# Down and w_out with tokens on the partitions: Strassen over 16 of 22 row blocks, norms along rows

## The chip, the cores and the metric

The kernel runs on one core of one Trainium2 chip. TensorE (PE) multiplies, VectorE (DVE) and ScalarE (ACT) work on tiles in SBUF and PSUM, GpSimd (POOL) helps, and SyncE (SP) and other engines' queues issue transfers (DMA). The metric is the device time of one execution in microseconds (us). The kernel before takes 2519.57 us, the median of 3 runs (2518.89 to 2524.14).

## The reference

Two layers of an encoder on 512 tokens with 1024 channels. Each layer has three sub-layers, and each of these has a norm ahead of it and one behind it:

```python
    for l in range(L):
        y = swiglu(rmsnorm(h, ffn1_pre_g[l]), ffn1_w_gu[l], ffn1_w_down[l])
        h = h + 0.5 * rmsnorm(y, ffn1_post_g[l])
        u = rmsnorm(h, mix_pre_g[l])
        proj = u @ w_in[l]
        ...
        merged = jnp.sum(gates * yb, axis=2)
        h = h + rmsnorm(merged @ w_out[l], mix_post_g[l])
        y = swiglu(rmsnorm(h, ffn2_pre_g[l]), ffn2_w_gu[l], ffn2_w_down[l])
        h = h + 0.5 * rmsnorm(y, ffn2_post_g[l])
```

`swiglu(x)` is `(silu(gate) * up) @ w_down`, where gate and up are the halves of `x @ w_gu`, 2816 columns each. The mixer between the FFNs projects to three kinds of attention with a sigmoid gate per branch and channel, and ends with `w_out`, 1024 by 1024. All is float32.

## The kernel before

Everything is kept transposed: features on the partitions, 512 tokens along the free axis. So h is 8 tiles of 128x512 and an FFN's activations are 22 such row blocks. A product with weights has the weight block (128x128) as the stationary operand and the activation (512 tokens) as the moving one. To keep float32 accuracy, each operand is split into a high part that TensorE takes exactly and a low rest, and each product is three matmuls (hi x hi, hi x lo, lo x hi; lines L246 to L248, `mm3`, and L650 in `product`).

Weights come from DRAM in the order of use as tiles of 512 KB (8 blocks of 128x128, tag `wr`, 3 buffers). `ensure` splits them, high by ScalarE (L201), low by VectorE (L202), 512 columns an instruction.

An FFN begins with 6 plain columns of gate and up (`PLAIN`), whose first 3 accumulators run in two token halves (`begin`), so that they can start when half of the tokens are ready. The other 16 of the 22 columns are Strassen products: the 8 input blocks and 512 tokens are cut in two each way, and seven products of 12 matmuls of 128x256 (L650) take the place of eight. Their weight sums are VectorE's (L543, L562, L572 and others). Down follows: 8 columns of 22 row blocks, seven whole (512 tokens) and the last in two token halves (`end`).

The norm behind it goes over features, and so over partitions: squares are summed on POOL and VectorE (L311), a matmul with ones sums the partitions (L291), the root and reciprocal make one number per token, and `spread` (L282) repeats it on all partitions by a matmul with the identity. `refresh` multiplies y by it (L413), adds y to h (L416, POOL and VectorE) and makes the next operand X (L316, L317) without the next norm, whose factor `rB` is multiplied in later (for instance L1051 at the gates). The first half of the tokens does this under the second half's products. w_out does the same, with 2 columns in halves. During the mixer h lies in DRAM (`kept`).

The order on each engine is that of a list scheduler of the framework, which takes the program's order and the buffers that are free. Tags name the buffers: `wr` raw weights, `x` split weights, `mm`, `at`, `o` PSUM banks.

Of the kernel before, what the change touches and what calls it, by code (L numbers as in the profile page):

```python
# [16 lines left out]
P = 128  # L17
# [12 lines left out]
TAIL_MIX = 2  # L30
AHEAD = 2
WARM = 9
PLAIN = 6
PAD = {"f": 184, "m": 184}
SECOND = 1
MIX_HOLD = ("g", "g", "g", "g", "g", "tx")[-TAIL_MIX * KD // 4 :]
KEEP_FF = 16
TAIL_FF = KF - KEEP_FF
PAD_FF = -TAIL_FF % 4
NBLOCKS = L * (  # L40
    2 * (2 * KF * KD + KF * KD + TAIL_FF + PAD_FF) + 54 * KD + 3 * 4 * KD + KD * KD
)
# [20 lines left out]
ROWN = ("diff_lambda_q1", "diff_lambda_k1", "diff_lambda_q2", "diff_lambda_k2", "sw_sink")  # L63
ROWW = 4 * 64 + 8
# [47 lines left out]
def encoder_kernel(ctx: ExitStack, tc: tile.TileContext, order, xT, wts, cols, rows, rpb, consts, tables, out):  # L112
# [9 lines left out]
    BUFS = {"h": 8, "x": 12, "t": 6, "wr": 3, "wp": 4}  # L122
    ABUFS = {"f": {}, "m": {"rr": 4, "tx": 5, "st": 16, "g": 10, "s": 2, "pt": 4}}
# [35 lines left out]
    nhalf = cp.tile([P, NCOLS], F32, tag="nhalf", name="nhalf")  # L159
# [46 lines left out]
    def wblk(name, l, r, c):  # L206
        n = len(order)
        if n % HB == 0:
            upto = n // HB + 1 + AHEAD
            if n // HB < stream["limit"]:  # L210
                upto = min(upto, stream["limit"])
            ensure(upto)
            for _ in range(min(stream["pace"], len(stream["later"]))):
                stream["later"].pop(0)()
            stream["tile"] = stream["ready"].pop(0)
        order.append((name, l, r, c))
        hi, lo = stream["tile"]
# [3 lines left out]
    h = [big("h", name="h") for _ in range(KD)]  # L221

    def load(hs, *bs):
        for b in bs:
            nc.sync.dma_start(h[b][:, hs], xT[b * P : (b + 1) * P, hs])

    G.memset(ones, 1.0)
    nc.scalar.dma_start(colt, cols)
    A.activation(dummy, ones[:, 0:1], AF.Copy)
    load(HALVES[0], 0)  # L230
    fetch(2, nc.sync)
    load(HALVES[0], 1, 2)
    fetch(1, nc.sync)
    load(HALVES[0], 3, 4, 5)
    fetch(1, nc.sync)
    load(HALVES[0], 6, 7)
    load(HALVES[1], *range(KD))
    nc.sync.dma_start(cons, consts)
    warm = bank("o")
    for _ in range(WARM):  # L240
        PE.matmul(warm[:, :P], ones, ones, start=True, stop=True)
    V.tensor_scalar(out=half, in0=colt, scalar1=0.5, scalar2=None, op0=ALU.mult)
    V.tensor_scalar(out=nhalf, in0=colt, scalar1=-0.5, scalar2=None, op0=ALU.mult)

    def mm3(acc, w, x, start, stop):
        PE.matmul(acc, w[0], x[0], start=start, stop=False)  # L246
        PE.matmul(acc, w[0], x[1], start=False, stop=False)  # L247
        PE.matmul(acc, w[1], x[0], start=False, stop=stop)  # L248

    def dense(blocks, X, tags=("mm",), cs=WHOLE, accs=None, ws=None, midway=None):  # L250
        accs = accs or [bank(tags[i % len(tags)]) for i in range(len(blocks))]
        n = len(X)
        kept = []
        for k in range(n):
            if midway and k == n // 2:
                midway()
            x = X[k][0][:, cs], X[k][1][:, cs]
            for i, (acc, (name, l, r0, c)) in enumerate(zip(accs, blocks)):
                w = ws[k * len(blocks) + i] if ws else wblk(name, l, r0 + k, c)
                kept.append(w)  # L260
                mm3(acc[:, cs], w, x, k == 0, k == n - 1)
        return (accs, kept) if cs == HALVES[0] else accs
# [49 lines left out]

    def operand(X, i, b, gcol):
        hs = HALVES[i]
        hi, lo = X[b]
        A.activation(hi[:, hs], h[b][:, hs], AF.Copy, scale=gcol(b))  # L316
        V.scalar_tensor_tensor(  # L317
            out=lo[:, hs], in0=h[b][:, hs], scalar=gcol(b), in1=f(hi)[:, hs], op0=ALU.mult, op1=ALU.subtract
        )

    def begin(refresh, X, first, spare):

        s = Squares()
# [869 lines left out]
```

## Time and profile before

| | |
|---|---|
| runs (median, range) | 2519.57 us, 2518.89 to 2524.14 |
| profiled execution | 2517.49 us, its span 2515.7 us |
| mean granted TensorE clock | 0.994 |
| busy: TensorE, VectorE, ScalarE, POOL | 98%, 68%, 50%, 8% of the span |
| layer 0, FFN1: gate and up by Strassen | about 75 to 240 us |
| its down product, its handover | about 240 to 360, 360 to 375 us |
| mixer | about 375 to 910 us |
| weight tiles | 415 of 512 KB, 3.5 us from issue to landing |

Row forms of the profile: a group's row gives line, engine, operation, output<-inputs, shape, count, then busy us and mean ns, then the idle time of the engine ahead of it and what ended it. A timeline row gives start and duration in us. A row of windows gives the stretch, its width, then busy us of each engine, the granted clock (PEclk, 1.00 is full), the share of the DMA engines and GB/s.

### The profile page before, as it was taken

Reading aid. Unit: us, or ns where it says so; the run is one execution under the profiler, and the core shown is the slowest. Engines: PE = TensorE matmul, PEld = TensorE weight load, DVE = VectorE, ACT = ScalarE, POOL = GpSimd, SP = SyncE. Lnnn points to the kernel's source line nnn. Section 1 sums busy time; section 2 is a strip of 40 time slices with the busy share of each in tenths; the row PEclk is TensorE's granted clock in tenths of the full one; section 3 lists DMA queues with packets and bytes.
Section 4 is the critical chain, followed back from the end, with each engine's and each line's share of the span. In section 5 each row is a group of like instructions: output and inputs, shape, how many; then the busy total and the mean of one; then the engine's idle time right before and its main releaser. Section 6 shows DMA issues by size and latency. Waiting matters only on the chain.

```text
span 2515.7 us, 38188 instructions
## 1 busy us (share of the span) xinstructions
PE 2471.4 (98%) x14586; PEld 2181.1 (87%) x14586; DVE 1702.3 (68%) x3062; ACT 1260.5 (50%) x2447; POOL 197.6 (8%) x177
## 2 busy tenths in 40 slices
PE   9999999999999999999999999999999999999998
PEld 8999888888778889998889998888787788899987
DVE  8877248857767478773388772588676764887723
ACT  6555245645555455553355553546455554555532
POOL 0000020000111120000100000200011112100002
PEclk9999999999999999999999999999999999999999
DMA  4333337434443323333233333374344423233232
GB/s 153 109 106 97 100 101 208 115 109 127 117 126 98 108 65 116 101 101 93 92 93 109 110 93 93 125 197 116 107 126 133 119 90 110 65 116 103 91 103 84
DMA packets 97398, 278.21 MB, mean 111 GB/s; under 512 B 13504, under 2 KB 17984, under 8 KB 97216
## 3 DMA queue, kind: packets, MB, share of 16 engines
q10 hardware_dynamic: 41184, 149.52, 19.5%
q1 hardware_dynamic: 56032, 126.27, 17.7%
q8 instruction: 114, 1.87, 0.3%
q14 instruction: 68, 0.56, 0.1%
HBM read 231.16 MB, written 6.29 MB: 94 GB/s over the span
## 4 chain that ended last, share of the span: by engine, by line
PE 85%; DVE 7%; DMA 4%; issue 1%; SPq 1%; ACT 1%; POOL 1%; POOLq 0%; DVEq 0%; ACTq 0%
PE mm L650 19%; PE mm L248 14%; PE mm L247 14%; PE mm L246 14%; PE at L246 4%; PE at L247 4%; PE at L248 4%; PE at L650 3%; DMA wr<-in_wts_dram 1%; DVE X L317 1%; DMA sh<-raw 1%; PE at L884 1%; DVE y L413 1%; PE at L856 1%; PE o L888 1%
## 5 line engine op out<-in xcount | busy, mean ns | idle before, releaser
L202 DVE TENSOR_TENSOR w<-wr,w 128x512 fp32r<-128x512 f32 x568 | 406.6, 721 | 408.7 <-ACT w L201 406.6
L201 ACT ACTIVATE w<-wr 128x512 fp32r<-128x512 f32 x568 | 354.3, 629 | 554.1 <-PE at L248 269.3
L248 PE MATMUL mm<-X,w 128*128 128x512 f32 (+1 forms) x1096 | 418.5, 383 | 7.2 <-DVE w L202 7.2
L247 PE MATMUL mm<-X,w 128*128 128x512 f32 (+1 forms) x1096 | 419.0, 383 | 4.2 <-DVE X L317 4.2
L246 PE MATMUL mm<-X,w 128*128 128x512 f32 (+1 forms) x1096 | 419.3, 384 | 2.9 <-ACT w L201 1.8
L650 PE MATMUL mm<-lt,h 128*128 128x256 f32 x1024 | 289.8, 283 | 0.0
L650 PE MATMUL mm<-ht,h 128*128 128x256 f32 x1024 | 289.8, 283 | 0.0
L650 PE MATMUL mm<-ht,l 128*128 128x256 f32 x1024 | 289.8, 283 | 0.0
L248 PEld LDWEIGHTS mm<-X,w 128*128 128x128 f32 x1096 | 209.8, 192 | 41.5 <-DVE w L202 8.4
L247 PEld LDWEIGHTS mm<-X,w 128*128 128x128 f32 x1096 | 210.1, 192 | 39.2 <-DVE X L317 6.4
L246 PEld LDWEIGHTS mm<-X,w 128*128 128x128 f32 x1096 | 210.0, 192 | 36.2 <-ACT w L201 2.0
L650 PEld LDWEIGHTS mm<-lt,h 128*128 128x128 f32 x1024 | 196.0, 191 | 0.0
L650 PEld LDWEIGHTS mm<-ht,l 128*128 128x128 f32 x1024 | 196.0, 191 | 0.0
L650 PEld LDWEIGHTS mm<-ht,h 128*128 128x128 f32 x1024 | 196.0, 191 | 0.0
L543 DVE TENSOR_TENSOR r<-wr,wr 128x1024 f32<-128x1024 f32 x64 | 78.5, 1226 | 117.9 <-DMA wr<-in_wts_dram 115.1
L311 POOL TENSOR_TENSOR ss<-ss,sq 128x512 f32<-128x512 f32 (+1 forms) x38 | 47.3, 1245 | 1357.6 <-ACT sq L310 1356.5
L247 PE MATMUL mm<-a,w 128*128 128x512 f32 (+1 forms) x432 | 152.7, 354 | 0.0
L650 PE MATMUL mm<-h,h 128*128 128x256 f32 x512 | 145.7, 285 | 3.4 <-DVE v L704 3.3
L650 PE MATMUL mm<-h,l 128*128 128x256 f32 x512 | 144.9, 283 | 0.0
L650 PE MATMUL mm<-l,h 128*128 128x256 f32 x512 | 144.9, 283 | 0.0
L271 ACT ACTIVATE hi<-at 128x256 fp32r<-128x256 f32 (+2 forms) x168 | 76.5, 473 | 73.1 <-PE at L884 29.4
L247 PE MATMUL mm<-lo,w 128*128 128x512 f32 (+1 forms) x288 | 110.6, 384 | 0.0
(270 smaller groups left out, 5814.7 us busy)
## 6 DMA issues: line engine op xcount, KB each, us to landing
wr<-in_wts_dram ACTq DMA_DIRECT2D x285, 512.0 KB, 3.5
wr<-in_wts_dram SPq DMA_DIRECT2D x130, 512.0 KB, 3.5
st<-hi SPq DMA_DIRECT2D x84, 128.0 KB, 2.4
st<-lo SPq DMA_DIRECT2D x84, 128.0 KB, 3.3
sh<-raw SPq DMA_DIRECT2D x104, 64.0 KB, 3.4
sw<-lo SPq DMA_DIRECT2D x36, 128.0 KB, 3.8
sw<-hi SPq DMA_DIRECT2D x36, 128.0 KB, 2.7
braw<-in_rpb_dram SPq DMA_DIRECT2D x16, 256.0 KB
```

What stands on the lines that cost most here:

```text
L201: A.activation(hi, raw, AF.Copy)
L202: V.tensor_tensor(out=lo, in0=raw, in1=f(hi), op=ALU.subtract)
L246: PE.matmul(acc, w[0], x[0], start=start, stop=False)
L247: PE.matmul(acc, w[0], x[1], start=False, stop=False)
L248: PE.matmul(acc, w[1], x[0], start=False, stop=stop)
L271: A.activation(hi, src, AF.Copy)
L311: eng.tensor_tensor(out=self.acc[:, cs], in0=self.acc[:, cs], in1=sq[:, cs], op=ALU.add)
L317: V.scalar_tensor_tensor(out=lo[:, hs], in0=h[b][:, hs], scalar=gcol(b), in1=f(hi)[:, hs], op0=ALU.mult, op1=ALU.subtract)
L413: V.tensor_tensor(out=y[b][:, hs], in0=y[b][:, hs], in1=reps[i], op=ALU.mult)
L543: V.tensor_tensor(out=W[g]["r13"], in0=base, in1=raws[g][0], op=ALU.add)
L650: PE.matmul(acc, ws[i], xs[j], start=start and k == n == 0, stop=stop and k == HK - 1 and n == 2, skip_group_check=True,)
L856: PE.matmul(sp, qs, sk[0][:, j0 * P : j1 * P], start=True, stop=False)
```

## The change

**Products.** In down and w_out the roles change: a block of 128 tokens of the activation is the stationary operand (128x128) and 512 columns of weights are the moving one, so the result has tokens on the partitions. Down has 4 token blocks and 2 column halves; w_out is 8 row blocks x 4 token blocks x 2 halves.

**Strassen in down.** 16 of the 22 row blocks form two halves of 8, the tokens two halves of 256 and the columns two of 512: seven products, in the order of `seq` (kinds 1, 7, 6, 4, 2, 5, 3), each of 4 units with two row blocks. The other 6 row blocks are straight products (n1 and n2, of 3 units each). The differences of activations that the products need are VectorE's (L882, L885) and are split by `cut` (L877). Of weights, kinds 7 and 5 need sums of two blocks, which a transfer with `accum_op` makes: issued from POOL, it adds the second block onto the first (L829, L832). Kinds 6 and 3 add on VectorE (L841). An FFN's down takes 42 tiles of 512 KB where it took 22. `loads` runs 6 steps ahead, `preps` (split, L850) 4 steps.

**Norms.** A token is a row now, so `Handover` sums squares along the row (Square with `accum_out`), makes one number per partition and multiplies it in with `scalar_tensor_tensor` (L407, L432). h is read from DRAM and written there at each sub-layer. Then TensorE transposes the normed rows, 4 blocks into one bank (L435), and the bank is split into the next X (L440). X comes normed, so `rB` remains only in the very first FFN. The three other FFNs take 4 plain columns and 18 by Strassen.

```diff
@@ -27,19 +27,15 @@
-PLAIN = 6
...
+KS = 8
+KP = KF - 2 * KS
+HOLD_OUT = ("g", "g", "g", "g", "g", "tx", "tx", "pt")
+DOWN_TILES = 42
...
-    BUFS = {"h": 8, "x": 12, "t": 6, "wr": 3, "wp": 4}
-    ABUFS = {"f": {}, "m": {"rr": 4, "tx": 5, "st": 16, "g": 10, "s": 2, "pt": 4}}
+    BUFS = {"X": 6, "n": 2, "wr": 3, "wp": 4}
+    ABUFS = {"f": {"t": 4, "x": 10}, "m": {"t": 5, "h": 4, "rr": 2, "tx": 5, "st": 16, "g": 10, "s": 2, "pt": 4}}
...
+    class Handover:
...
+        def take(self, tb, n, src):
+            junk = big("t", name="junk")
+            A.activation(junk, src, AF.Square, accum_out=self.ss[tb][:, n : n + 1])
+            V.tensor_tensor(out=self.value(tb, n), in0=src, in1=self.g1[n], op=ALU.mult)
+
+        def rms(self, ss):
+            r = small("rh", 1, 8)
+            V.tensor_tensor(out=r, in0=ss[:, 0:1], in1=ss[:, 1:2], op=ALU.add)
+            A.activation(r, r, AF.Sqrt, scale=1.0 / D, bias=epst)
+            V.reciprocal(out=r, in_=r)
+            return r
+
+        def merge(self, tb):
+            r = self.rms(self.ss[tb])
+            s2 = small("sh", 2, 8)
+            for n in range(2):
+                y, h = self.value(tb, n), self.hold(tb, n)
+                V.scalar_tensor_tensor(out=h, in0=y, scalar=r, in1=h, op0=ALU.mult, op1=ALU.add)
+                if self.following:
+                    junk = big("t", name="junk")
+                    A.activation(junk, h, AF.Square, accum_out=s2[:, n : n + 1])
+            if not self.following:
...
+            d = dr.tile([P, D], F32, tag="kept", name=nm("kept"), bufs=2 * NT)
+            for n in range(2):
+                nc.sync.dma_start(d[:, n * T : (n + 1) * T], self.hold(tb, n))
+            kept[tb] = d
+            r = self.rms(s2)
+            if self.X is None:
+                self.X = Operand(self.raw)
+            for n in range(2):
+                x = self.value(tb, n)
+                V.scalar_tensor_tensor(out=x, in0=self.hold(tb, n), scalar=r, in1=self.g2[n], op0=ALU.mult, op1=ALU.mult)
+                tp = bank(self.tags[n])
+                for k in range(HB):
+                    PE.transpose(tp[:, k * P : (k + 1) * P], x[:, k * P : (k + 1) * P], ident)
+                src = tp.rearrange("p (k t) -> p k t", k=HB)
+                ts = slice(tb % 2 * P, tb % 2 * P + P)
+                hi, lo = self.X.hi[n][:, tb // 2, :, ts], self.X.lo[n][:, tb // 2, :, ts]
+                A.activation(hi, src, AF.Copy)
+                V.tensor_tensor(out=lo, in0=src, in1=f(hi), op=ALU.subtract)
...
+        UNITS, LAST = KS // 2, KP // 2
+        seq = [(k, u) for k in ("1", "7", "n2", "6", "4", "n1", "2", "5", "3") for u in range(LAST if k[0] == "n" else UNITS)]
...
+        def load(s):
+            kind, u = seq[s]
+            if kind == "7":
+                rS[u] = z(("ht3", "lt3", "ht2", "lt2")[u], F32)
+                nc.sync.dma_start(rS[u], wblock(0, u, 1))
+                G.dma_start(rS[u], wblock(0, u, 0), accum_op=ALU.add)
+            elif kind == "5":
+                wraw[s] = plain_load(0, u, 1)
+                G.dma_start(wraw[s], wblock(1, u, 1), accum_op=ALU.add)
+            else:
+                half, n = {"1": (0, 0), "2": (1, 0), "3": (1, 0), "4": (1, 1), "6": (1, 1), "n1": (None, 0), "n2": (None, 1)}[kind]
+                wraw[s] = plain_load(half, u, n)
+
+        def prep(s):
+            kind, u = seq[s]
+            src = wraw.pop(s, None)
+            if kind in "63":
+                V.tensor_tensor(out=rS[u], in0=rS[u], in1=src, op=ALU.add)
+            if kind in "763":
+                src = rS[u]
+            h, q = pair("wh"), pair("wl")
+            if kind == "n2":
+                A.activation(h, src, AF.Copy, scale=-1.0)
+                V.scalar_tensor_tensor(out=q, in0=src, scalar=-1.0, in1=f(h), op0=ALU.mult, op1=ALU.subtract)
+            else:
+                A.activation(h, src, AF.Copy)
+                V.tensor_tensor(out=q, in0=src, in1=f(h), op=ALU.subtract)
+            wsplit[s] = h, q
...
+        def seven(s, accs, start, stop, tbs=(0, 1)):
+            kind, u = seq[s]
+            w = wsplit[s]
+            for k in range(2):
+                for tb in tbs:
+                    x = tuple(tok(t, 2 * u + k, tb) for t in forms[kind])
+                    unit(
+                        accs[tb], x, (w[0][:, k, :], w[1][:, k, :]), start and u == k == 0,
+                        stop and u == UNITS - 1 and k == 1,
+                    )
...
+        def first_rows():
+            t = z("ap", F32, (P, KP, T))
+            kept_v["v11"], kept_v["v12"] = t[:, 0:2, :], t[:, 2:4, :]
+            for tb in range(2):
+                hand[0].take(tb, 0, b[tb])
+            for tb in range(2):
+                hand[0].merge(tb)
+
+        def second_rows():
+            plus("v22", a)
+            copies("v12", None, a)
+            for tb in (2, 3):
+                hand[0].take(tb, 1, kept_v["v22"][:, tb - 2, :])
...
+        job("5", 0, first_rows)
+        job("3", 0, second_rows)
+
+        for s, (kind, u) in enumerate(seq):
+            loads(s + 6)
+            preps(s + 4)
+            for call in jobs.get(s, ()):
+                call()
...
+            elif kind == "3" and u == 0:
+                preps(len(seq))
+                assert len(order) == len(stream["raw"]) * WB
+                stream["made"] = 2 * len(stream["raw"])
+                forms["3"] = forms["3x"]
+                if following:
+                    ensure(stream["made"] + 2)
+                for tb in range(2):
+                    for i in range(UNITS):
+                        seven(s + i, e, False, True, (tb,))
+                    t = kept_v["v12"][:, tb, :]
+                    V.tensor_tensor(out=t, in0=e[tb], in1=t, op=ALU.add)
+                    hand[0].take(2 + tb, 0, t)
+                    if following:
+                        ensure(stream["made"] + 1)
+                    hand[0].merge(2 + tb)
+        return hand[0].X
...
+        accs = [bank("at") for _ in range(3)] + [bank("o")]
+        for k in range(KD):
+            wq = wquad("w_out", l, k, 0)
+            for tb in range(NT):
+                mm3(accs[tb], rows_of(k, tb), wq, k == 0, k == KD - 1)
+            ensure(min(stream["made"] + 1, at + 2 * KD))
+        ws = [wquad("w_out", l, k, HB) for k in range(KD)]
+        last = [bank("mm") for _ in range(NT)]
+        for tb in range(NT):
+            for k in range(KD):
+                mm3(last[tb], rows_of(k, tb), ws[k], k == 0, k == KD - 1)
+            if tb == 0:
+                for i in range(NT):
+                    hand.take(i, 0, accs[i])
+            hand.take(tb, 1, last[tb])
+            ensure(at + 2 * KD + tb + 1)
+            hand.merge(tb)
+        return hand.X
```

Lines L266 to L268 of the new kernel are L246 to L248 of the old; L966 is the new product (`unit`).

The first place is TensorE's queue at the end of FFN1 of layer 0, where the next sub-layer's first products begin. Before (X are the next operand's tiles, `ss` the summed squares, `rs` the reciprocal roots; `mm_3682` and `mm_3684` are accumulators of the first token half):

```order
L247 MATMUL mm_3682<-X_3442,w_3638 128x256
L291 MATMUL o_3666<-ones,ss_2963 128x1 x2
L248 MATMUL mm_3682<-X_3442,w_3638 128x256
L246 MATMUL mm_3684<-X_3442,w_3638 128x256
L247 MATMUL mm_3684<-X_3442,w_3638 128x256
```

Now (`o_3280` is the last product of down, `ap` and `ht` hold the normed rows of the two last token blocks, `at_3765`, `at_3767` and `mm_3766` the accumulators of the first token half):

```order
L966 MATMUL o_3280<-wh_3606,f3x_3312 128x512
L266 MATMUL at_3765<-X_3484,w_3622 128x256
...
L268 MATMUL at_3765<-X_3486,w_3723 128x256
L435 MATMUL mm_3680<-cons,ap_3459 128x128 x4
L435 MATMUL mm_3688<-cons,ht_2987 128x128 x4
L435 MATMUL mm_3745<-cons,ap_3459 128x128 x4
L435 MATMUL mm_3753<-cons,ht_2987 128x128 x4
L266 MATMUL mm_3766<-X_3484,w_3622 128x256
```

The norm's small matmuls stood between products of the first token half. Now 33 of that half's 72 matmuls stand ahead of the 16 transposes of the last two token blocks, and 39 behind them.

The second place is VectorE's queue in the middle of the down product of the same FFN. Before, all of it is splits of weights (`w`):

```order
L202 TENSOR_TENSOR w_2916<-wr_2914,w_2916 128x512
L202 TENSOR_TENSOR w_2931<-wr_2914,w_2931 128x512
L202 TENSOR_TENSOR w_2948<-wr_2946,w_2948 128x512
L202 TENSOR_TENSOR w_2972<-wr_2946,w_2972 128x512
L202 TENSOR_TENSOR w_2989<-wr_2987,w_2989 128x512
```

Now (`wl` is the low part of a weight, `ht`, `lt` and `a` sums of weights and differences of activations, `f` their low parts, `part` the straight blocks' low parts):

```order
L539 TENSOR_TENSOR part_2963<-ap_459,part_2961 128x512
L841 TENSOR_TENSOR ht_2774<-ht_2774,wr_2930 128x1024
L841 TENSOR_TENSOR lt_2795<-lt_2795,wr_2954 128x1024
L885 SCALAR_TENSOR_TENSOR ht_2752<-ht_2752,a_1991 128x1024
L850 TENSOR_TENSOR wl_2984<-ht_2774,wh_2983 128x1024
L850 TENSOR_TENSOR wl_3020<-lt_2795,wh_3019 128x1024
L885 SCALAR_TENSOR_TENSOR lt_2791<-lt_2791,a_2468 128x1024
L841 TENSOR_TENSOR ht_2822<-ht_2822,wr_2980 128x1024
L877 TENSOR_TENSOR f_3057<-ht_2752,f_3056 128x1024
L877 TENSOR_TENSOR f_3057<-lt_2791,f_3056 128x1024
```

Two splits per tile of 512 KB became one of twice the width, and sums, differences and cuts stand between them.

The third place is POOL's queue over the same FFN. Before, it adds squares (L311) and then h (L416), 18 instructions, of which these are the first of each:

```order
L311 TENSOR_TENSOR ss_2963<-ss_2963,sq_2966 128x512
...
L416 TENSOR_TENSOR h_74<-h_74,y_2756 128x256
```

Now it issues eight adding transfers and nothing else:

```order
L829 DMA ht_2774<-in_wts_dram 128x1024
L829 DMA lt_2795<-in_wts_dram 128x1024
L829 DMA ht_2822<-in_wts_dram 128x1024
L829 DMA lt_2841<-in_wts_dram 128x1024
L832 DMA wr_3341<-in_wts_dram 128x1024
L832 DMA wr_3378<-in_wts_dram 128x1024
L832 DMA wr_3397<-in_wts_dram 128x1024
L832 DMA wr_3416<-in_wts_dram 128x1024
```

Over the whole program TensorE's matmuls of 128x512 go from 6256 to 6136, those of 128x256 from 7216 to 7000, the 128x128 ones from 607 to 785 and the ones-matmuls from 80 to 36. VectorE's instructions go from 2975 to 2884, ScalarE's from 2509 to 2343.

More of the change, by code (lines that the diff above doesn't have):

```diff
@@ L311, in add, with finish_rms, begin @@
             eng.tensor_tensor(out=self.acc[:, cs], in0=self.acc[:, cs], in1=sq[:, cs], op=ALU.add)
[L313 to L323, printed above, removed]
+    def finish_rms(s, rB):
+        V.tensor_copy(rB, inv_rms(s.acc, D, NT))
+    def begin(X, first, spare, between=None):
         assert len(order) % HB == 0
@@ L973, in attn_a @@
                 )
[L974 removed]
+            OT["a", p] = tuple(t[:, p, :] for t in oa)
+            A.activation(OT["a", p][0], o, AF.Copy)
+            V.tensor_tensor(out=OT["a", p][1], in0=o, in1=f(OT["a", p][0]), op=ALU.subtract)
         def bias_b(i):
```

678 lines of the change are left out of this document (410 added, 268 removed).

## The prediction

> **What bounds the kernel now.** I read the page first (shares, then the chain of waits), then windows by stage, then the timeline for the spacing of TensorE's matmuls.
>
> ```profile
> span 2515.7 us, 38188 instructions
> PE 2471.4 (98%) x14586; PEld 2181.1 (87%) x14586; DVE 1702.3 (68%) x3062; ACT 1260.5 (50%) x2447; POOL 197.6 (8%) x177
> PE 85%; DVE 7%; DMA 4%; issue 1%; SPq 1%; ACT 1%; POOL 1%; POOLq 0%; DVEq 0%; ACTq 0%
> ```
>
> TensorE is busy for 98% of the span and 85% of the chain. So a matmul that disappears is worth its own spacing, unless another engine cannot follow. Which engine that could be, the windows say:
>
> ```profile
> core 0: us, PE busy (x) PEld busy (x) DVE busy (x) ACT busy (x) POOL busy (x), PEclk, DMA share, GB/s
> 75.00:240.00 165.00, 164.11 (x1356) 163.30 (x1355) 129.69 (x170) 90.34 (x160) 0.00 (x0) 1.00 0.34 103
> 240.00:360.00 120.00, 119.89 (x590) 101.67 (x589) 42.66 (x68) 42.80 (x75) 11.44 (x11) 1.00 0.31 97
> 360.00:375.00 15.00, 12.61 (x81) 12.20 (x80) 12.10 (x30) 8.26 (x23) 2.76 (x5) 0.77 0.33 104
> 910.00:970.00 60.00, 59.53 (x307) 50.91 (x306) 53.35 (x83) 30.07 (x50) 1.47 (x2) 1.00 0.29 88
> 1240.00:1270.00 30.00, 27.48 (x214) 26.80 (x213) 21.30 (x47) 16.93 (x39) 9.94 (x13) 0.94 0.21 69
> 1600.00:1640.00 40.00, 35.98 (x284) 34.59 (x283) 32.19 (x73) 23.08 (x54) 10.01 (x13) 1.00 0.52 169
> 880.00:920.00 40.00, 37.73 (x277) 36.11 (x276) 27.96 (x63) 24.98 (x58) 14.67 (x17) 0.96 0.17 55
> 2140.00:2180.00 40.00, 37.72 (x253) 34.80 (x252) 32.65 (x74) 22.09 (x51) 10.06 (x13) 0.96 0.13 41
> ```
>
> 75 to 240 is gate and up by Strassen products, 240 to 360 the down product, and the rows from 360:375 on, but for 910:970, hold a handover from one sub-layer to the next: three after an FFN (360, 1240, 1600) and two after w_out (880, 2140). The down product is the emptiest stage: VectorE has 42.66 of 120 us to do. The handovers are where TensorE loses time. Idle time plus what the lower clock costs, (width - busy) + (1 - PEclk) x busy, gives 2.4 + 2.9 = 5.3, 2.5 + 1.6 = 4.2 and 4.0 us after the FFNs (mean 4.5), and 3.8 and 3.8 us after w_out.
>
> **The change part by part: TensorE's sum.** The spacing of matmuls in an unbroken stretch is their price; for groups of x2 or more, the timeline gives one duration from first start to last end.
>
> ```profile
> 199.74 0.28 PE L650 MATMUL mm<-ht,l 128*128 128x256 f32 x1
> 199.86 0.28 PE L650 MATMUL mm<-ht,h 128*128 128x256 f32 x1
> 299.78 0.39 PE L248 MATMUL mm<-l,w 128*128 128x512 f32 x1
> ...
> 301.59 0.39 PE L247 MATMUL at<-ht,w 128*128 128x512 f32 x1
> 666.77 0.27 PE L1027 MATMUL at<-cons,s 128*128 128x128 f32 x1
> 421.50 0.49 PE L884 MATMUL at<-cons,s 128*128 128x128 f32 x3
> 353.34 0.61 PE L291 MATMUL o<-ones,ss 128*128 128x1 f32 x4
> 353.81 0.36 PE L248 MATMUL mm<-h,w 128*128 128x256 f32 x1
> 354.64 0.71 PE L282 MATMUL at<-cons,rs 128*128 128x128 f32 x4
> 355.11 0.36 PE L248 MATMUL mm<-l,w 128*128 128x256 f32 x1
> ```
>
> So a 256-wide matmul costs 0.12 us. A 512-wide one costs 0.227 (from 299.78 to 301.59 eight steps in 1.81 us). Three fp32 128x128 transposes end 0.49 after the first started, of which one alone lasts 0.27: 0.11 each. A ones or spread matmul of the norms leaves two records; 353.34 to 353.81 and 354.64 to 355.11 hold two each: 0.235 each. The counts are those of the two instruction orders.
>
> Down, per FFN: now 462 512-wide and 132 256-wide matmuls, 104.9 + 15.8 = 120.7 us; then 336 in the seven products and 144 straight ones, all 512-wide: 480 x 0.227 = 109.0. That is -11.7, four times: -47.0. Strassen on 16 of 22 blocks would save 1/8 of 16/22 = 9%, and the rest is the lost halves of the tail. w_out: 144 x 0.227 + 96 x 0.12 = 44.2, then 192 x 0.227 = 43.6: -0.6 twice, -1.2. Three FFNs move two column pairs from plain to Strassen: 96 x 0.227 = 21.8 against 168 x 0.12 = 20.2, -1.6 thrice: -4.9. Norms: 44 ones and 44 spreads less, 88 x 0.235 = -20.7. Transposes of h and X: 224 x 0.11 = +24.6. Together **-49.2 us**. All of this lies on the path, for TensorE is it.
>
> **VectorE and the transfers in the down stage.** This is what must stay hidden behind the 109 us.
>
> ```profile
> L543 DVE TENSOR_TENSOR r<-wr,wr 128x1024 f32<-128x1024 f32 x64 | 78.5, 1226 | 117.9 <-DMA wr<-in_wts_dram 115.1 <-PE mm L248 2.8
> L572 DVE TENSOR_TENSOR wr<-wr 128x512 f32<-128x512 f32 x64 | 44.2, 691 | 1.9
> L507 DVE SCALAR_TENSOR_TENSOR a<-h,colt,h 128x512 f32<-128x512 f32 x32 | 22.9, 746 | 0.0
> L547 ACT ACTIVATE h<-wr 128x1024 fp32r<-128x1024 f32 x64 | 67.6, 1057 | 28.6 <-PE mm L650 28.0 <-DMA wr<-in_wts_dram 0.5
> L201 ACT ACTIVATE w<-wr 128x512 fp32r<-128x512 f32 x568 | 354.3, 629 | 554.1 <-PE at L248 269.3 <-PE mm L248 258.1 <-DMA wr<-in_wts_dram 10.8
> L869 ACT ACTIVATION_READ_ACCUMULATOR s<-s,nmx 128x1 f32 x128 | 24.1, 188 | 0.0
> ```
>
> Between the first split of a down tile and the last down matmul VectorE's order holds 34 splits, 8 weight sums, 12 cuts and 8 differences, 62 x 1.226 = 76 us, and some 31 ops on 512 columns (settles, bank sums, row norms), 22 us; with the small ones 100 us, and some 8 more that spill over from the last gate products: 100 to 108 us against TensorE's 109 plus the transposes there, 112. That is 90 to 96%. ScalarE has 34 x 1.06 and less than 50 us beside: no bound. The nearest row is 910:970, where VectorE is busy for 53.35 of 60 us (89%) and TensorE lost 0.5 us. From below the price is 0. From above, if VectorE cannot do better than that 89%, 108 / 0.89 = 121 us, 9 more than 112. I take 2 per FFN, nearer the row in which nothing was lost: **+8**, ends 0 and +36.
>
> ```profile
> GB/s 153 109 106 97 100 101 208 115 109 127 117 126 98 108 65 116 101 101 93 92 93 109 110 93 93 125 197 116 107 126 133 119 90 110 65 116 103 91 103 84
> wr<-in_wts_dram ACTq DMA_DIRECT2D x285, 512.0 KB, 3.5
> out_dram<-h SPq DMA_DIRECT2D x16, 128.0 KB, 1.7
> ```
>
> The stage fetches 42 tiles of 512 KB in some 112 us, 197 GB/s where it had 97; a slice with 208 exists, so the rate alone is no stall. Eight of the 42 are added onto their target by transfers issued from POOL, and no row shows such a transfer. From below one costs what the nearest row shows, 3.5 us. From above twice that, 7, because it also reads its target. Four (kind 7) go to buffers of their own and are needed 13 to 24 us after their issue, so even 4 x 7 = 28 in a row is late by 4 at most. Four (kind 5) share three buffers: per tile a plain load 3.5, the add, and a split 1.06 + 1.23; with an add of 7 this is 12.8 x 4/3 = 17 us where four steps of TensorE take 4 x 12 x 0.227 = 10.9, and the splits run four steps (10.9) ahead. So either end costs nothing that is not in the +8; I take 0, ends 0 and +4 per FFN. POOL no longer adds h and squares there, so nothing stands before them in its queue. In a sentence by itself: the Trainium skill, "DMA: Bandwidth & Descriptors", Anatomy of one DMA, gives transfers of this path 2.0 us + bytes / 436e3, an estimate of 3.2 us here, and by it the sum stays as it is.
>
> **The handovers.** After the last product of a token block come, in a chain: bank sum 0.69, Square 0.63 + 0.19, a small add, root and reciprocal 0.54 together, two gain-and-add ops of 0.75, Square again 0.82, 0.54, two of 0.75, four transposes 0.44, copy 0.63, subtract 0.69, and a dozen hops: about 10 us. By the order VectorE's queue puts 12 us of work into that stretch, since the splits of the next weights and the other block's rows stand between. TensorE has 33 matmuls of 0.12 and eight transposes ready, 4.9 us; the other 39 of the first token half (4.7 us) stand behind the waiting transposes in its queue. So 6 to 8 us idle, and a lower clock behind it:
>
> ```profile
> 363.98 0.28 PE L247 MATMUL mm<-X,w 128*128 128x256 f32 x1
> 365.79 0.80 PE L248 MATMUL mm<-X,w 128*128 128x256 f32 x2 [1.52 <-DVE w L202]
> 366.38 0.41 PE L246 MATMUL mm<-X,w 128*128 128x256 f32 x1
> 366.59 0.41 PE L247 MATMUL mm<-X,w 128*128 128x256 f32 x1
> 372.06 0.28 PE L248 MATMUL mm<-X,w 128*128 128x256 f32 x1
> ```
>
> After a gap of 1.52 us the matmuls stand 0.21 apart instead of 0.12 for some 6 us, 2.5 us lost; at 1600 the clock stayed at 1.00 through 4.0 us of idle time. I take 7 + 1 = 8 per FFN, where there were 4.5: **+10.5** for three. After w_out the same chain, with 1.8 us of product to cover it but fewer rows between: 6.5 for 3.8, **+5.4** for two. Ends: the cover holds (4 each, -2) and nothing covers (12 each, +39). In sentences of their own: the Trainium skill, "TensorE: Matmul & The Clock Gate", The HAM clock gate, says that the clock falls to half when the engine was not busy over a window of about 3.4 us; with a longer gap at each handover every one would pay the 2.5 that only the first shows in full, and the sum would be 7 us higher. The row at 1600 speaks against it, the one at 360 for it.
>
> **Mixer and end.** X comes normed, so the gates and values need no multiplication by the row scale:
>
> ```profile
> L1051 DVE TENSOR_TENSOR gate<-mm,rB 128x512 f32<-128x512 f32 x48 | 33.0, 687 | 25.5 <-PE mm L248 18.9 <-POOL gate L1063 6.2
> 2503.57 0.28 PE L248 MATMUL mm<-l,w 128*128 128x256 f32 x1
> 2503.95 0.38 ACT L310 ACTIVATE sq<-mm 128x256 f32<-128x256 f32 x1 [4.46 <-PE mm L248]
> 2504.37 0.43 DVE L311 TENSOR_TENSOR ss<-ss,sq 128x256 f32<-128x256 f32 x1 [1.18 <-ACT sq L310]
> ```
>
> That frees VectorE of 33 us in two mixers, off the path but for the softmax chains: 0 to -8, I take **-4**. The end takes 12.1 us from 2503.57 to the end of the span. The new one: sum 0.69, Square 0.82, 0.54, two of 0.75, eight transposes 0.88, a copy 0.69, the store 1.7, hops 1: about 8.5 to 9. **-3**, ends 0 and -4.
>
> **The sum**: -49.2 + 8 + 10.5 + 5.4 - 4 - 3 = -32.3. The profiled execution took 2517.5 us, 1.8 more than its span; the new one should take 2485, and as the median of the runs stands 2.1 above the profiled one, **2487** as runs are timed.
>
> **The rivals.** (A) *VectorE becomes the bound of the down stage*: at 89% and 108 us each takes 9 instead of 2, +28, and with the handovers at 10 another +6 to +8: about 2522, no change, in a band from 2502 to 2535. For it: the load goes from 36% to over 90%, and a queue in order stalls on every late tile. Against it: 910:970. (B) *The accumulating transfers are slow*, one mechanism on the other side: it decides where one of them takes more than about 6 us in a row of four, because the fourth of kind 7 is needed 24 us after issue. At 12 each (a little over three plain landings) kind 7 is 24 late and kind 5 passes its cover of 21.8 us by 2 ((5.8 + 12) x 4/3 = 23.7): +26 per FFN, 104 in all, 2591, slower. For it: no row has one, and each waits for a plain load first; against it, DMA is used at 0.31 there. (C) *All is hidden*: handovers as now, nothing lost in the down stage: 2517.5 - 49.2 - 4 - 3 + 2 = 2463. For it: the down stage starts with splits four steps ahead; against it, the queue position of the 39 matmuls. That the change does not remove the matmuls is excluded by the counts.
>
> **How the numbers follow.** Forecast, 2472 to 2502, 45%; C, below 2472, 20%; A 20%; B 15%. A change under 0.2%, 5 us, cannot be told from none. Faster by more: 45 + 20 and half of A, 75%; same: a quarter of A and a rest, 6%; slower: B and the upper end of A, 19%. Range 2458 to 2535: it leaves out B (15%) and the lowest 4% or so of C; the likeliest's own is 2472 to 2502.
>
> **What would show it.** Right: TensorE's busy time near 2425 us; windows over the down stage with VectorE at 90% or more and TensorE at 97% or more; 6 to 9 us lost per FFN handover, ended by VectorE's row ops ahead of the transposes; the accumulating transfers landing in under 7 us. Wrong: matmuls of the seven products waiting for a split whose releaser is a transfer issued by POOL (B), or for VectorE all along the stage (A); a spacing other than 0.227 with activations as the stationary side.

## The result: slower by 1%, and the profile after

The changed kernel takes 2547.4 us (2542.0 to 2548.6, 4 runs) against 2519.2 us of the kernel before in the same runs: a ratio of 1.0105, with a 95% interval from 1.0084 to 1.0125. Faster by 1.3% was forecast, and the time lies above the range of 2458 to 2535 as well. Lines of the page and of the transfers, with the median us from issue to landing at a transfer row's end:

```profile
span 2540.2 us, 37714 instructions
...
PE 2441.3 (96%) x14298; PEld 2144.3 (84%) x14298; DVE 1800.9 (71%) x2935; ACT 1350.1 (53%) x2471; POOL 114.7 (5%) x96
...
q0 software_dynamic: 4608, 16.78, 3.6%
...
PE 78%; DMA 8%; DVE 8%; ACT 3%; issue 2%; SPq 1%; POOL 1%; ACTq 0%; POOLq 0%; DVEq 0%
...
wr<-in_wts_dram POOLq DMA_DIRECT2D x16, 512.0 KB, 7.5
...
ht<-in_wts_dram POOLq DMA_DIRECT2D x8, 512.0 KB, 11.0
lt<-in_wts_dram POOLq DMA_DIRECT2D x8, 512.0 KB, 12.4
```

TensorE has less to do, as the prediction worked out, yet its share fell from 98 to 96%, and in the chain of waits transfers rose from 4 to 8%. The queue q0 is new: it holds the 32 adding transfers, which land after 7.5 to 12.4 us where plain ones of the same size take 3.5 to 4.2. Windows over the first FFN's down stage and its handover show where TensorE stood still (columns as before: busy us of TensorE, its weight loads, VectorE, ScalarE, POOL, then the clock, the DMA share and GB/s):

```profile
240.00:275.00 35.00, 29.15 (x136) 24.25 (x136) 28.45 (x28) 18.81 (x23) 3.01 (x4) 0.91 0.72 196
275.00:345.00 70.00, 70.00 (x309) 58.00 (x308) 41.92 (x41) 28.50 (x34) 3.45 (x4) 1.00 0.71 207
345.00:385.00 40.00, 28.16 (x141) 24.02 (x140) 33.87 (x62) 23.32 (x54) 0.00 (x0) 0.83 0.45 148
```

In the middle of the stage TensorE lost nothing, and there VectorE was busy for only 42 of 70 us. All the loss is at the two ends. To compare it over the whole program I add up, for each stretch, the time between the starts of two TensorE instructions less their unbroken spacing (0.227, 0.120 and so on); this counts idle time and the slower clock together.

| lost TensorE time, us | before | after |
|---|---|---|
| in down, ahead of kind 6 (four FFNs: 7.6, 9.6, 9.8, 7.9) | 0 | 34.9 |
| in down, at the first transposes (8.2, 7.2, 5.1, 7.5) | 0 | 28.0 |
| three FFN handovers | 17.9 | 27.7 |
| two w_out handovers | 10.3 | 18.4 |
| two mixers | 38.5 | 38.0 |
| start, end and other | 14.0 | 11.4 |
| sum | 80.7 | 158.4 |

The unbroken spacings themselves sum to 2424.5 us before and 2376.5 after, 48.0 less. From the start of the last TensorE instruction to the end of the span it was 9.1 us, now 4.3. So 77.7 - 48.0 - 4.8 = +24.9 us, and the spans differ by 24.5.

**The first place, ahead of kind 6.** The timeline of the changed kernel (start, duration; in brackets the idle time before and what ended it):

```profile
248.76 1.06 ACT L849 ACTIVATE wh<-ht 128x1024 fp32r<-128x1024 f32 x1 [4.79 <-DMA ht<-in_wts_dram]
252.64 1.06 ACT L849 ACTIVATE wh<-lt 128x1024 fp32r<-128x1024 f32 x1 [2.83 <-DMA lt<-in_wts_dram]
...
257.92 1.06 ACT L849 ACTIVATE wh<-lt 128x1024 fp32r<-128x1024 f32 x1 [1.40 <-DMA lt<-in_wts_dram]
...
249.85 1.23 DVE L850 TENSOR_TENSOR wl<-ht,wh 128x1024 fp32r<-128x1024 f32 x1 [3.77 <-ACT wh L849]
...
253.74 1.23 DVE L850 TENSOR_TENSOR wl<-lt,wh 128x1024 fp32r<-128x1024 f32 x1 [1.52 <-ACT wh L849]
...
259.02 1.23 DVE L850 TENSOR_TENSOR wl<-lt,wh 128x1024 fp32r<-128x1024 f32 x1 [1.18 <-ACT wh L849]
...
269.31 1.22 DVE L841 TENSOR_TENSOR ht<-ht,wr 128x1024 f32<-128x1024 f32 x1
...
270.62 1.06 ACT L849 ACTIVATE wh<-ht 128x1024 fp32r<-128x1024 f32 x1 [4.59 <-DVE ht L841]
271.58 1.07 ACT L1000 ACTIVATE ht<-mm 128x512 f32<-128x512 f32 x2
...
265.98 0.39 PE L966 MATMUL o<-wh,part 128*128 128x512 f32 x1
272.21 0.79 PE L966 MATMUL mm<-wh,part 128*128 128x512 f32 x1 [5.85 <-ACT ht L1000]
```

ScalarE waits for the tiles of kind 7, which the adding transfers complete, and VectorE waits for ScalarE: 3.77 + 1.52 + 1.18 = 6.5 us without work. TensorE does not wait for kind 7 itself; those splits come in time. But VectorE's queue runs 6.5 us late from here on without a gap, its sum for kind 6 comes at 269.31, and ScalarE stands 4.59 us for it, ahead of kind 6's split (270.62). Behind this split in ScalarE's queue is a copy that empties a PSUM bank (L1000). TensorE needs that bank within the straight products n2, which come just before kind 6: it runs out of other work after the product at 265.98 and stands for 5.85 us.

**The second place, at the first transposes.**

```profile
337.54 1.06 ACT L849 ACTIVATE wh<-wr 128x1024 fp32r<-128x1024 f32 x1 [4.95 <-DMA wr<-in_wts_dram]
342.31 1.06 ACT L849 ACTIVATE wh<-wr 128x1024 fp32r<-128x1024 f32 x1 [3.71 <-DMA wr<-in_wts_dram]
343.27 0.58 ACT L392 ACTIVATE junk<-at 128x512 f32<-128x512 f32 x1
...
344.54 0.68 DVE L393 TENSOR_TENSOR ap<-at,ht 128x512 f32<-128x512 f32 x1
...
354.87 0.74 DVE L432 SCALAR_TENSOR_TENSOR ap<-a,rh,lt 128x512 f32<-128x512 f32 x1
...
349.84 0.39 PE L966 MATMUL at<-wh,f3x 128*128 128x512 f32 x1
355.66 1.11 PE L435 MATMUL mm<-cons,ap 128*128 128x128 f32 x4 [5.43 <-DVE ap L432]
```

Again no product waits for its weights. ScalarE waits 4.95 and 3.71 us for tiles of kind 5, and behind the second one stands the first Square of the row norm (L392). The norm's chain starts late (by 6.4 us, as a run below shows), VectorE works through kind 3's sums and splits between the chain's steps, and TensorE, whose queue has the first four transposes amid products that are ready, stands for 5.4 us.

### The profile page after: what moved, and what is told of

It reads as the page before. It is cut to its first block, busy times and chain, and to the rows that moved or that the text cites. A ratio compares the mean times of both kernels' runs of the same rounds, so it can differ in the third digit from the quotient of the medians.

```text
span 2540.2 us, 37714 instructions
## 1 busy us (share of the span) xinstructions
PE 2441.3 (96%) x14298; PEld 2144.3 (84%) x14298; DVE 1800.9 (71%) x2935; ACT 1350.1 (53%) x2471; POOL 114.7 (5%) x96
## 3 DMA queue, kind: packets, MB, share of 16 engines
q10 hardware_dynamic: 26208, 94.98, 12.4%
## 4 chain that ended last, share of the span: by engine, by line
PE 78%; DMA 8%; DVE 8%; ACT 3%; issue 2%; SPq 1%; POOL 1%; ACTq 0%; POOLq 0%; DVEq 0%
PE mm L737 23%; PE mm L268 9%; PE mm L267 9%; PE mm L266 9%; PE mm L966 5%; PE at L737 4%; DMA wr<-in_wts_dram 3%; DMA lt<-in_wts_dram 3%; PE at L966 2%; PE at L266 2%; PE at L267 2%; PE at L268 2%; PE o L966 1%; PE at L1185 1%; DMA sh<-raw 1%
## 5 line engine op out<-in xcount | busy, mean ns | idle before, releaser
L200 DVE TENSOR_TENSOR w<-wr,w 128x512 fp32r<-128x512 f32 x360 | 256.1, 718 | 179.8 <-ACT w L199 178.7
L266 PE MATMUL mm<-X,w 128*128 128x512 f32 (+1 forms) x980 | 379.6, 387 | 2.1 <-ACT w L199 1.6
L267 PE MATMUL mm<-X,w 128*128 128x512 f32 (+1 forms) x980 | 379.5, 387 | 0.1
L268 PE MATMUL mm<-X,w 128*128 128x512 f32 (+1 forms) x980 | 378.7, 387 | 0.0
L199 ACT ACTIVATE w<-wr 128x512 fp32r<-128x512 f32 x360 | 222.7, 627 | 236.3 <-PE mm L268 173.6
L266 PEld LDWEIGHTS mm<-X,w 128*128 128x128 f32 x980 | 186.4, 190 | 33.9 <-ACT w L199 2.1
L268 PEld LDWEIGHTS mm<-X,w 128*128 128x128 f32 x980 | 186.2, 190 | 30.8
L737 PE MATMUL mm<-X,h 128*128 128x256 f32 x1120 | 207.7, 283 | 0.0
L966 PE MATMUL mm<-wh,f 128*128 128x512 f32 x640 | 200.2, 391 | 0.0
L850 DVE TENSOR_TENSOR wl<-wr,wh 128x1024 fp32r<-128x1024 f32 x76 | 93.1, 1225 | 119.0 <-ACT wh L849 118.8
L737 PEld LDWEIGHTS mm<-X,h 128*128 128x128 f32 x1120 | 175.0, 192 | 0.3
L737 PE MATMUL mm<-X,l 128*128 128x256 f32 x560 | 158.7, 283 | 0.0
L600 DVE TENSOR_TENSOR l<-wr,h 128x1024 fp32r<-128x1024 f32 x70 | 85.7, 1224 | 89.1 <-PE mm L737 89.1
L966 PEld LDWEIGHTS mm<-wh,f 128*128 128x128 f32 x640 | 120.6, 189 | 24.8
```

Source lines behind the costliest of these rows:

```text
L199: A.activation(hi, raw, AF.Copy)
L200: V.tensor_tensor(out=lo, in0=raw, in1=f(hi), op=ALU.subtract)
L600: V.tensor_tensor(out=W[g]["l1"], in0=raws[g][0], in1=f(W[g]["h1"]), op=ALU.subtract)
L737: PE.matmul(acc, ws[i], xs[j], start=start and k == n == 0, stop=stop and k == HK - 1 and n == 2, skip_group_check=True,)
L850: V.tensor_tensor(out=q, in0=src, in1=f(h), op=ALU.subtract)
L966: PE.matmul(acc, x[i], w[j], start=start and n == 0, stop=stop and n == 2, skip_group_check=True)
```

## The experiments

My theory after this reading (T): the adding transfers are late, and what they cost is paid by the work queued behind the waiting splits on ScalarE and VectorE. The rivals: VectorE simply has too much to do (V, the forecast's rival A); the transposes stand too early in TensorE's queue whatever comes in time (W); it is POOL's queue or the second transfer per tile, not the adding.

**Both kinds of adding transfers left out.**

```diff
-                G.dma_start(rS[u], wblock(0, u, 0), accum_op=ALU.add)
+                wblock(0, u, 0)
...
-                G.dma_start(wraw[s], wblock(1, u, 1), accum_op=ALU.add)
+                wblock(1, u, 1)
```

> Both kinds of adding transfers are left out (16 + 16 of kind 7 and 5 over the four FFNs; the second block of each sum is not loaded, so these two products are those of one block); every instruction of the engines stays. Theory T (late transfers hold back the in-order queues of ScalarE and VectorE): TensorE's idle time ahead of kind 6 (34.9 us over the four FFNs) and ahead of the first transposes (28.0 us) mostly goes, 50 to 63 us less, 2485 to 2500 us. Rival V (VectorE has too much to do): its instructions are the same, so the time stays within 8 us of 2547.

Measured: 2480.3 us, 67 less than the changed kernel and 5 below the range given for T, 0.985 of the time before (0.983 to 0.988). Its windows:

```profile
240.00:275.00 35.00, 35.00 (x167) 29.44 (x167) 34.78 (x34) 22.55 (x27) 0.00 (x0) 1.00 0.49 162
275.00:330.00 55.00, 55.00 (x244) 45.54 (x243) 34.30 (x34) 23.66 (x29) 0.00 (x0) 1.00 0.62 197
330.00:375.00 45.00, 38.59 (x212) 33.75 (x211) 36.41 (x66) 24.72 (x56) 0.00 (x0) 0.89 0.54 170
```

TensorE is busy for all of 35 us while VectorE is busy for 34.78 of them: VectorE at 99% holds nothing up. Both places are gone (at most 0.6 us lost in each of the four down stages); the handovers stay, 28.1 and 18.0 us. Rival V falls at the first place, where VectorE's work is the same instruction for instruction and in the same order. W is not decided by this run: without kind 5's adding transfers the list scheduler ordered the work around the second place anew, and in TensorE's queue the first transposes stand four products (0.9 us) later than in the changed kernel, nine in the last FFN.

**Only kind 7's, and only kind 5's, left out**: the first half, and then the second half, of the diff above.

> Only the adding transfers of kind 7 are left out (the second block is not loaded). T: the place ahead of kind 6 goes (30 to 35 us less, 2512 to 2518), the one ahead of the first transposes stays at about 28 us. V: no change.

> Only the adding transfers of kind 5 are left out. T: the place ahead of the first transposes shrinks by 15 to 28 us (2520 to 2532), the one ahead of kind 6 stays at about 35. V, and a rival W (the transposes simply stand too early in TensorE's queue for the chain of row operations): both stay, 2540 or more.

Measured: 2509.2 us without kind 7's (38 less than the changed kernel), 2514.0 without kind 5's (33 less). Without kind 7's the first place is empty in all four FFNs and the second still costs 7.3 to 9.0 us a time; without kind 5's it is the other way round (8.1, 8.1, 9.3, 9.2 us ahead of kind 6). Together the two savings make 72, against 67 for both at once. Each time is below the range that I gave (2512 to 2518, 2520 to 2532): the places answered as T says, but I had set their price too low. Without kind 7's the three engines' orders are those of the changed kernel; without kind 5's the order around the second place is that of the run before, so part of its 33 us may be the order's. Without kind 5's, ScalarE's timeline around the first Square reads:

```profile
334.55 1.06 ACT L849 ACTIVATE wh<-wr 128x1024 fp32r<-128x1024 f32 x1 [1.66 <-PE at L966]
336.87 0.60 ACT L392 ACTIVATE junk<-at 128x512 f32<-128x512 f32 x1 [1.26 <-PE at L966]
```

ScalarE waits for TensorE here, not for a transfer, and the Square starts at 336.87 where it started at 343.27, 6.4 us earlier, though in this run the first place is as it was. That start lies ahead of anything that the scheduler moved. Each kind of transfer has its place.

**The same transfers without the adding.**

```diff
-                G.dma_start(rS[u], wblock(0, u, 0), accum_op=ALU.add)
+                G.dma_start(rS[u], wblock(0, u, 0))
...
-                G.dma_start(wraw[s], wblock(1, u, 1), accum_op=ALU.add)
+                G.dma_start(wraw[s], wblock(1, u, 1))
```

> The same transfers from POOL's queue, with the same bytes and the same order, but they write over the first block and do not add. If it is the adding that is slow, landing falls from 11 to 13 us to about 5 and the time to that of the run without these transfers, 2485 to 2505. If it is the queue, or two transfers in a row for each tile, landing stays above 9 us and the time above 2535.

Measured: 2498.4 us, 49 of the 67 us gone. The profile of line L829 (kind 7) and L832 (kind 5), first of the changed kernel, then of this run (the time that the issue takes on POOL in ns, then landing in us):

```profile
L829 POOL DMA_DIRECT2D ht<-in_wts_dram x8: 853/862/997, 239.4 to 2402.9; - x8
...
DMA to landing us min/median/max: 8.5/12.3/14.3
...
L832 POOL DMA_DIRECT2D wr<-in_wts_dram x16: 853/861/865, 319.3 to 2493.9; - x16
...
DMA to landing us min/median/max: 5.6/7.5/8.1
```

```profile
L829 POOL DMA_DIRECT2D ht<-in_wts_dram x8: 527/528/669, 239.1 to 2372.8; - x8
...
DMA to landing us min/median/max: 6.6/8.2/9.9
...
L832 POOL DMA_DIRECT2D wr<-in_wts_dram x16: 527/528/530, 315.3 to 2460.5; - x16
...
DMA to landing us min/median/max: 3.6/4.0/5.3
```

The adding makes a transfer of 512 KB land 3.5 to 4 us later, 7.5 instead of 4.0 alone and 12.3 instead of 8.2 where four are under way. Of both expectations neither holds whole: the time is in the first one's range, but kind 7's landing fell to 8.2 and not to 5, and 18 us stay over the run without these transfers, for the second transfer of each tile and, at the second place, perhaps for the order there. But the adding is the larger part. This is also the cleanest test of T: TensorE, VectorE and ScalarE have all the instructions of the changed kernel in the same order, and with nothing but the adding gone the first place falls from 34.9 to about 13 us and the second from 28.0 to about 11. So W falls for the larger part of the second place: the transposes stand where they stood.

**The sums on POOL, from plain transfers.**

```diff
-                G.dma_start(rS[u], wblock(0, u, 0), accum_op=ALU.add)
+                t = plain_load(0, u, 0)
+                G.tensor_tensor(out=rS[u], in0=rS[u], in1=t, op=ALU.add)
...
-                G.dma_start(wraw[s], wblock(1, u, 1), accum_op=ALU.add)
+                t = plain_load(1, u, 1)
+                G.tensor_tensor(out=wraw[s], in0=wraw[s], in1=t, op=ALU.add)
```

> The eight sums per FFN are made by plain transfers of both blocks and an add on POOL (128x1024, 2.5 us each by the 1.245 us that 128x512 took on POOL), so the computation is whole again. Theory T (it is the adding transfer's time that holds the queues): near the run without the transfers, 2485 to 2500 us; the plain second transfers keep some of the 18 us that the run with overwriting transfers still lost. Rival V (VectorE): POOL's adds slow VectorE's two-input instructions, and the time comes out above 2515.

Measured: 2568.8 us, 1.019 of the time before (1.015 to 1.023), the slowest of all: T's figure missed, the rival's part on VectorE came true. VectorE and POOL in its timeline:

```profile
244.85 2.40 POOL L830 TENSOR_TENSOR ht<-ht,wr 128x1024 f32<-128x1024 f32 x1 [243.88 <-DMA wr<-in_wts_dram]
247.21 2.84 POOL L830 TENSOR_TENSOR lt<-lt,wr 128x1024 f32<-128x1024 f32 x1
...
243.78 1.22 DVE L852 TENSOR_TENSOR wl<-wr,wh 128x1024 fp32r<-128x1024 f32 x1
244.91 2.88 DVE L539 TENSOR_TENSOR part<-ap,part 128x512 fp32r<-128x512 f32 x1
247.72 3.41 DVE L879 TENSOR_TENSOR f<-ht,f 128x1024 fp32r<-128x1024 f32 x1
```

A VectorE instruction that reads two SBUF operands beside such an add takes 2.88 us instead of 0.69, and 3.41 instead of 1.22: longer by 2.2, about POOL's own 2.4, as if it ran after it. Four in a row cost VectorE 8.8 us, more than the 6.5 us for which it waited on the adding transfers, and the first place is back (6.0 to 6.3 us lost at each stop, 41 us in all with the slower clock behind it). The second place grew too, from 28 to 43 us, and the three handovers from 28 to 33; this run does not separate what made those. The Trainium skill, "SBUF — State Buffer", Who interferes with whom, says that a VectorE instruction with two SBUF inputs contends with a GpSimd instruction that reads SBUF, because the second input comes through a read interface that the two share, and calls the shared ports an exclusive lock; these rows agree.

**The sums on VectorE, from plain transfers**: the same edit with `V.tensor_tensor`.

> The eight sums per FFN are made by plain transfers and an add on VectorE, 8 x 1.22 = 9.8 us more of its work per FFN, the computation is whole. T: VectorE has that time (42 of 70 us busy in the middle of the down stage), so 2485 to 2505 us. V: 10 us more per FFN of an engine at its limit would give 2547 + 0 to 40 us, in any case above 2525.

Measured: 2505.5 us, 0.994 of the time before (0.992 to 0.996), the computation whole. VectorE takes on 8 x 1.22 us per FFN and the program gets 42 us faster than the changed kernel, against V's 2525 or more. The first place is gone, but not by the transfers alone. VectorE's sum for kind 6 starts at 266.93, where it started at 262.26 without any second block, and kind 6's split on ScalarE at 268.20; TensorE needs the bank at 265.4. What saves it is that the scheduler put the bank's copy, which in the changed kernel stood behind this split, ahead of it (263.64). In the old order the copy would have ended near 269.7, so by an estimate from these rows TensorE would have stood some 4 us. At the first transposes a stop of 2.4 to 2.8 us is left in each FFN, and the row of kind 5's sums suggests why (its idle time ahead: 44.5 us, ended by transfers):

```profile
L834 DVE TENSOR_TENSOR wr<-wr,wr 128x1024 f32<-128x1024 f32 x16 | 19.6, 1226 | 44.5 <-DMA wr<-in_wts_dram 44.5
```

Each sum needs two of the three buffers `wr` at once, and VectorE waits for the second tile.

**Kind 5 without a second load.** After kind 6 the running sum holds the first block and the two that kind 5 wants, so kind 5 is that sum less the first block.

```diff
-                wraw[s] = plain_load(0, u, 1)
-                G.dma_start(wraw[s], wblock(1, u, 1), accum_op=ALU.add)
+                wraw[s] = plain_load(0, u, 0)
...
+            if kind == "5":
+                V.tensor_tensor(out=src, in0=rS[u], in1=src, op=ALU.subtract)
             if kind in "763":
```

> Kind 7 is summed by a plain transfer and VectorE as in the run before. Kind 5's sum is not loaded twice: after kind 6 the running sum holds three blocks, and VectorE subtracts the first block (one plain transfer) from it, so an FFN loads 38 tiles where it loaded 42, with the same 8 sums on VectorE. The computation is whole. Theory T (the late tiles of kind 5, two loads through three buffers, hold the queues in front of the first transposes): the 3 us that are left ahead of the first transposes in each FFN go, 2484 to 2496 us, below the run with eight plain double loads. Rival: those 3 us are VectorE's extra sums; then 2497 to 2506 as there.

Measured: 2485.2 us (2480.5 to 2485.8), 0.986 of the time before (0.984 to 0.988), 62 us below the changed kernel, inside T's range, and the fastest of the kernels whose computation is whole. Its windows:

```profile
240.00:275.00 35.00, 35.00 (x165) 29.38 (x165) 34.02 (x34) 19.32 (x24) 0.00 (x0) 1.00 0.62 207
275.00:340.00 65.00, 65.00 (x288) 53.83 (x287) 52.56 (x56) 33.86 (x46) 0.00 (x0) 1.00 0.62 215
340.00:385.00 45.00, 38.15 (x243) 34.31 (x242) 32.75 (x64) 22.89 (x51) 0.00 (x0) 0.92 0.53 158
```

TensorE is full through the down stage, at 97 and 81% of VectorE and at 215 GB/s. What is left over the run without any second block is 5 us, and the intervals of the two ratios overlap. The eight sums on VectorE are still here, so they did not make the last 3 us a time; the late tiles are what remains. But the two kernels differ in the scheduler's order as well (in the run before, the first transposes stand five products earlier in TensorE's queue, and the three handovers lose 33 us against 27 here), so the 20 us between them are not all the tiles'. Against the changed kernel the second place is a clean comparison: from the first Square on, TensorE, VectorE and ScalarE have the same order in the first FFN, the Square starts at 329.00 where it started at 343.27, and the first transposes wait 0.28 us where they waited 5.43. At the first place the bank's copy stands ahead of kind 6's split, as in the run before (263.66 and 268.11), and that, not the transfers alone, keeps it empty.

## Why the prediction was wrong, point by point

**TensorE's sum, -49.2**: right, 48.0 by the spacings of the new trace. Its busy time was to be near 2425 us; the changed kernel shows 2441, but there the clock was lower after each stop, and without the adding transfers it is 2424.5.

**The down stage, +8 with ends 0 and +36; accumulating transfers, 0 with ends 0 and +4 per FFN**: this failed; 62.9 us were lost there. The price of one transfer was bounded at 7 us and measured 7.5 for kind 5, which is near; for kind 7 it was 8.5 to 14.3, with four under way at once. But what the step needed was four in a row, for which it allowed 28 us, and the first FFN's four had landed 18.4 us after the first was issued (239.42 to 257.84; 17.9 to 19.5 in the others). So the price set how much was lost (49 of 67 us went with the adding), but it is not where the step broke. The step asked whether the tiles would be late *for TensorE's products*, found four steps of cover and concluded that nothing was lost, and so far it held: no product of kinds 7 and 5 waited. It did not ask what stands behind the waiting split in ScalarE's and VectorE's queues. There it was kind 6's sum, with the bank's copy behind kind 6's split, and the first Square, and these had no four steps of cover: TensorE needs the copy within n2, three steps before kind 6, and the norm's chain by the first transposes. The same step worked out 17 us for four tiles of kind 5 against 10.9 of TensorE and saw the difference as covered; the first and the last of their four splits start 15.3 us apart (326.97 to 342.31), which are three steps, or 20 us for four at that rate.

**VectorE at 90 to 96%** did not come: in the changed kernel it was busy for 70.4 of the 105 us from 240 to 345, 67%. And where it was at 99%, in the run without the adding transfers, it held nothing up (rival A falls). VectorE's idle time, not its work, made the first gap.

**Rival B**, the accumulating transfers, had the right place and the right sign, at 15%, but another mechanism. It took the four transfers as one after the other, at 12 us each, so that the fourth comes after its 24 us and products wait: 104 us. Each did take 12.3 at the median, but they overlapped, all four landed in 18.4 us, and no product waited; the 67 us came by the queues.

**The handovers, +10.5 and +5.4**: 27.7 - 17.9 = +9.8 and 18.4 - 10.3 = +8.1. The 6 to 8 us of idle time came as forecast, in two pieces, ahead of the transposes of the last two token blocks:

```profile
375.58 0.63 PE L435 MATMUL mm<-cons,ap 128*128 128x128 f32 x4 [1.93 <-DVE ap L432]
376.16 0.66 PE L435 MATMUL mm<-cons,ht 128*128 128x128 f32 x4
381.30 1.09 PE L435 MATMUL mm<-cons,ap 128*128 128x128 f32 x4 [4.49 <-DVE ap L432]
```

The releaser is the row chain on VectorE, as the step said. After w_out the same two pieces stand, so fewer rows between did not shorten them, and +5.4 was 2.7 too low.

**Mixer, -4**: -0.5. VectorE lost 33 us of gate work there and TensorE gained next to nothing; what makes the softmax chains' waits these runs do not show. **End, -3**: from the last product to the end of the span 9.8 us where there were 12.1, -2.3.

**The sum without the failed step.** 2487 was forecast with a loss of 8 us in the down stage. The last kernel, in which the adding transfers are replaced, loses some 4 us there over the four FFNs and takes 2485.2. So the other terms held together, in part by luck: the mixers (3.5 us) and w_out (2.7) came out worse than forecast and the down stage 4 better, and this kernel has its first place empty by the scheduler's order. Still, the miss of 60 us is about what the failed step lost, 62.9.

## What to carry to other kernels

When a transfer gets slower, don't stop at the consumer of its data: list what is queued behind the instruction that waits for it, on every engine that runs in order, and ask when that is needed. VectorE at 99% with its inputs in time cost nothing here; ScalarE, busy for 18.8 of the 35 us in which the first place lies, stood in front of late tiles, and over both places and four FFNs this cost 63 us. Look at the order of the queue as well: a bank's copy ahead of a waiting split instead of behind it kept TensorE going in two of these kernels. And where a scheduler makes the order, compare the order before an experiment is read as one change. Where a sum of two loads is wanted, look for an algebraic way that loads less (a sum that is already there, less one block) before moving the adding to another engine.

## What the runs showed of the hardware that I had not expected

- An adding transfer of 512 KB from POOL's queue lands 7.5 us after its issue where the same transfer without adding takes 4.0 (medians of 16), and its issue holds POOL for 0.86 us instead of 0.53. With four under way it is 12.3 against 8.2. The Trainium skill, "DMA: Bandwidth & Descriptors", Anatomy of one DMA, gives 2.0 us + bytes / 436e3 for this path, an estimate of 3.2 us; that is 0.8 under the plain one here, and the adding one takes more than twice as long.
- An add on POOL with two SBUF operands delays VectorE's two-operand instructions by about its own length (2.88 us instead of 0.69 beside an add of 2.40), so POOL's idle time was not free.
- After the long stops the clock is low, after a short one it was not: four transposes take 1.11 and 1.09 us behind the stops of 5.43 and 4.49 us, and 0.63 behind that of 1.93. The loss from the clock is part of every place in the table. The row at 1600 us of the kernel before, which I set against the rule of the Trainium skill ("TensorE: Matmul & The Clock Gate", The HAM clock gate), has its 4.0 us of idle time in pieces of at most 1.5, so it was no evidence against it; these three stops agree with the rule. The row at 360, which I set for it, is no evidence either: stops of 0.87 and 1.52 us stand there, but alike at 1256 and 1616 us, and the two matmuls behind them take 0.80, 0.80 and 0.51 us. What decides after such short stops these rows leave open.
